# One pass over the second chunk, modulation from PSUM on ACT, and early products of a second FFN group

## The chip, the cores and the metric

The kernel runs on one core of a Trainium2 chip. The metric is the time of one execution on the device in microseconds (us), given as the median of several executions. The core has five engines that matter here: PE (TensorE, matrix products), DVE (VectorE), ACT (ScalarE), POOL (GpSimd) and SP (SyncE, which issues the loads). Each engine runs its own queue in order; semaphores between the engines make an instruction wait for its inputs and for a free buffer.

## The reference, cut to what matters

Two layers work on 1024 rows of 1024 values. Layer 0 mixes the rows by differential attention, layer 1 by centred averages over 2, 4, 8 and 16 neighbours. After each mixer comes a SwiGLU feed-forward network (FFN) with 2816 hidden values. Each of the four sub-layers modulates its input by a scale and a shift, is gated, added to its input and normalised.

```python
def modulate(h, shift, scale):
    return h * (1 + scale) + shift

def swiglu(h, w_in, w_out):
    g, u = jnp.split(h @ w_in, 2, axis=-1)
    return (jax.nn.silu(g) * u) @ w_out

for i in range(DEPTH):
    sh1, sc1, g1, sh2, sc2, g2 = adaln_params(c[:, None, :], w_mod[i], b_mod[i])
    hx = modulate(x, sh1, sc1)
    # y_lat: attention with w_o (layer 0), multiscale_pool(hx, pool_w, pool_scale) (layer 1)
    x = layer_norm(ALPHA * x + g1 * y_lat, ln_g[i, 0], ln_b[i, 0])
    x = layer_norm(ALPHA * x + g2 * swiglu(modulate(x, sh2, sc2), w_in[i], w_out[i]),
                   ln_g[i, 1], ln_b[i, 1])
```

## The kernel before

The state x lies transposed in SBUF as `zT`: 8 tiles of 128 features by 1024 rows. The rows are handled in two chunks of 512. Every fp32 product is made of three fp32r matmuls (`mm3`): an operand is cut into a high part, a cast on ACT (L386), and a remainder, a subtraction on DVE or POOL (L387); `parts` does both. Weights come by DMA into a ring `raw` of RAW = 4 buffers and are cut into a ring `aop` of AOP = 3 by `form`. `ct` is a ring of CT = 5 buffers for partial results, `quad` one of QD = 4.

After attention the stages follow one another:

- w_o, the attention's output product (`w_o`, L677 to L707). The first chunk is one pass of 512 columns over 8 output tiles d; the second is two passes of 256, each with its own weight forms.
- FFN of layer 0 (`ffn`, L709 to L874), in 11 groups of 2 x 128 hidden values. Both chunks are multiplied together by a Strassen-like scheme with 7 products per half (p0 to p6, gate half s = 0 and linear half s = 1), each of 12 matmuls of 512 columns. Their inputs H[0] to H[6] are seven forms of the modulated x: H[0] and H[1] come from the first chunk alone, the others also from the second chunk. At the end of a group 16 output products of 6 matmuls each add its share to zT. In group 0 and in the last group the two halves go product by product (p0 of both, then p1 of both, ...); in the others half after half.
- pooling (`pool_group`), again one pass of 512 and two of 256, with 4 groups each; then the FFN of layer 1, and the last norm.

Between a mixer and its FFN the rows are normalised (`ln_rows`): PE transposes 128 rows (L558), DVE takes mean and variance, POOL the power (L564), ACT writes the normalised rows `xn` (L568). `features` transposes them back (L587), `to_x` writes x into zT on ACT (L591), `modulated` makes the modulated h from zT on DVE (L595), and `put` cuts a form into its parts. Of the second chunk, row tiles 4 and 5 are handled in the mixer's last pass (`second_x`, `forms_rest`), tiles 6 and 7 in group 0 between p0 and p1; `forms_4` and `forms_last` complete the forms in group 0. `beside(g)` puts a vector-matrix product for layer 1's modulation (`gemv`, 4 loads, 8 DVE operations and 4 matmuls) at the end of a group.

What stands first on an engine's queue is settled when the kernel is built, from the order of the code and the rings of buffers; nothing is reordered at run time.

Of the kernel before, what the change touches and what calls it, by code (L numbers as in the profile page):

```python
# [19 lines left out]
P = 128  # L20
# [18 lines left out]
RAW, AOP, CT, QD = 4, 3, 5, 4  # L39
# [4 lines left out]
def backbone(ctx: ExitStack, tc: tile.TileContext, a: dict, out: bass.AP):  # L44
# [78 lines left out]
    with ExitStack() as actx:  # L123
# [420 lines left out]
    def quad(dt=F32R):  # L544
        return pf.tile([P, 2, 512], dt, name="quad", tag="quad", bufs=QD)
# [51 lines left out]
    def put(H, i, s, cs, t, eng=None):  # L597
        parts(H[s][:, i, cs], H[s][:, 4 + i, cs], t, eng)

    def forms_first(li, M, H, rows, ks):  # L600

        if not H:
            H += [h_form(0), h_form(1), phx.tile([P, KT, 512], F32, name="h", tag="x0"), None, None, None, None]
        for k in ks:
            to_x(k, chunk[0], li, features(rows, k))
            modulated(H[2][:, k, :], k, chunk[0], M)
            put(H, k % 4, k // 4, chunk[0], H[2][:, k, :], G)

    def second_x(li, rows, t0, ks=range(KT)):

        for k in ks:
            to_x(k, slice(512 + t0, 512 + t0 + 256), li, features(rows, k))

    def forms_rest(M, H, t0, idx):

        if H[5] is None:
            H[5:7] = [h_form(s) for s in range(5, 7)]
        cs, zs = slice(t0, t0 + 256), slice(512 + t0, 512 + t0 + 256)
        for i in idx:
            k = i + 4  # L620
            t2, h21 = H[2][:, i, cs], H[2][:, k, cs]
            t = quad(F32)
            h12, h22, t4 = t[:, 0, 0:256], t[:, 0, 256:512], t[:, 1, 0:256]
            modulated(h12, i, zs, M)
            modulated(h22, k, zs, M)
# [3 lines left out]
            G.tensor_tensor(t4, h21, t2, ALU.subtract)  # L629
            put(H, i, 5, cs, h12)  # L630
            put(H, i, 6, cs, t4, G)

    def forms_4(H):
        H[4] = h_form(4)
        for i in range(4):
            put(H, i, 4, chunk[0], H[2][:, i, :])

    def forms_last(M, H):

        H[3] = h_form(3)  # L640
        ts = [quad(F32) for _ in range(4)]
        for i, t in enumerate(ts):
            modulated(t[:, 0], i + 4, chunk[1], M)
            V.tensor_tensor(t[:, 1], t[:, 0], H[2][:, i, :], ALU.subtract)
            put(H, i, 3, chunk[0], t[:, 1])
        H[2] = h_form(2)
        for i, t in enumerate(ts):
            put(H, i, 2, chunk[0], t[:, 0], G)
# [6 lines left out]
    def ffn_mod(l):  # L655

        return one_plus(l, 4, f"m1_{l}"), modv[l][:, 24:32]
# [18 lines left out]
    M0 = ffn_mod(0)  # L676
# [21 lines left out]
    for d in range(KT):  # L698
        w_o(d, 512, 256)
        if d >= 2:  # L700
            forms_first(0, M0, H, rows, [range(0, 2), range(2, 4), [4], [5], [6], [7]][d - 2])
    rows = rows_of(4, 6)
    for d in range(KT):
        w_o(d, 768, 256)
        if 1 <= d < 5:
            second_x(0, rows, 0, (d - 1, d + 3))
            forms_rest(M0, H, 0, [d - 1])  # L707

    def ffn(l, gate, li, M, H, beside=None, after=None):  # L709
        class Half:  # L710


            def __init__(self, j0, s, sg):
                self.s, self.sg = s, sg
                self.r0, self.r1 = [raw([P, KT, P]) for _ in range(2)]
                for i, r in enumerate((self.r0, self.r1)):
                    SP.dma_start(r, a["w_in"][l, j0 + i, :, s])
# [94 lines left out]
        for g in range(G2):  # L812
            last = g == G2 - 1
            sg = []
            if g == 0 or last:
# [4 lines left out]
                if not last:  # L820
                    second_x(li, rows_of(6, 8), 256)
                sg0 = ct()
                o = [h.p1_(ct() if h.s else None, sg0) for h in both][1]
                if last:
                    keep = phh.tile([P, 2, 2, 512], F32R, name="keep", tag="H0")
                    for j in range(2):
                        S.copy(keep[:, j], at[1][j])
                else:
                    forms_rest(M, H, 256, range(4))
                    forms_4(H)  # L830
                for h in both:
                    h.sums(G if last else V)
                for h in both:
                    h.p4()
                for h in both:
                    h.p5()
                if not last:
                    forms_last(M, H)
                sg += [quad(F32), quad(F32)]
                at = [both[0].at(o)]  # L840
                for f in (Half.p6, Half.p3, Half.p2):
                    at.append([f(h) for h in both][1])
            else:
                sg += [quad(F32), quad(F32)]
                for s in range(2):
                    h = Half(2 * g, s, sg)
                    h.p0()
                    h.sums()
                    h.p4()
                    at = [h.p1_(h.p1)]  # L850
                    h.p5()
                    at += [h.p6(), h.p3(), h.p2()]
# [32 lines left out]

    ffn(0, g2, 0, M0, H, beside=lambda g: gemv(1, g + 2) if g < 10 else None, after=ln_to_pool)

# [4 lines left out]
    M2 = ffn_mod(1)  # L892
# [5 lines left out]
    def pool_group(t0, n, g):  # L898
        wr = raw([P, 2, 256])
        SP.dma_start(wr, a["pool_w"][g].rearrange("(i p) o -> p i o", p=P))  # L900
        if n == 512:
            pt = phx.tile([P, 6, 512], F32R, name="pt", tag=f"x{g % 3}")
        elif t0 == 512:
            pt = phx.tile([P, 6, 512], F32R, name="pt", tag=f"x{1 + g % 2}")
        else:
            pt = [pwt.tile([P, 2, 512], F32R, name="pt", tag="aop", bufs=AOP) for _ in range(2)]
        if t0 == 768:
            w2, hl = pt[0], pt[1].rearrange("p s (i t) -> p (s i) t", i=2)
        else:
            w2, hl = pt[:, 0:2], pt[:, 2:6]  # L910
# [36 lines left out]
    rows = []  # L947
# [12 lines left out]

# [94 lines left out]
```

## Time and profile before

| | us |
|---|---|
| median of 3 runs (2364.8 to 2369.83) | 2365.12 |
| the profiled execution | 2363.8 |
| its span, first to last instruction | 2362.0 |
| PE busy in it | 2258.1 (96%) |
| DVE busy | 1691.5 (72%) |
| ACT busy | 933.0 (40%) |
| POOL busy | 615.5 (26%) |

The mean granted clock of TensorE is 0.984 of full speed. Of the chain that ended last, PE has 84%, DVE 10%, ACT, DMA, POOL and issue 1% each. Matmuls are pipelined, so a matmul's own duration is longer than the distance from its start to the next one's start; the distance is what counts. A busy share is a mean over stages with different limits, so the stages are to be read one by one.

### The profile page before, as it was taken

The page shows a single profiled execution, that of the slowest core. Times are in us where ns is not written, and L with a number is a line of the kernel's source. Part 1 is how long each engine was busy: PE and PEld are TensorE (multiplying, and loading weights), DVE is VectorE, ACT ScalarE, POOL GpSimd, SP SyncE. Part 2 cuts the span into 40 slices and gives each one's busy share as a digit, 9 for nine tenths or more (in the row PEclk, how much of TensorE's full clock was granted, in tenths as well). Part 3 has the DMA queues.
Part 4 walks back from the last instruction along what each step waited for, and adds up shares of the span by engine and source line. Part 5 has one row for each costly group of instructions (what it writes and reads, how often), then busy time and mean ns, then how long its engine had stood idle before and what let it go on. Part 6 is the DMA issues. An engine that isn't in the chain of part 4 may idle for free.

```text
span 2362.0 us, 31120 instructions
## 1 busy us (share of the span) xinstructions
PE 2258.1 (96%) x11832; PEld 1922.8 (81%) x11832; DVE 1691.5 (72%) x2572; ACT 933.0 (40%) x1635; POOL 615.5 (26%) x618
## 2 busy tenths in 40 slices
PE   5989999999999987999999999998799999999997
PEld 4868887999998876888888888897588888888886
DVE  6663626998996689777777777757966666666678
ACT  3213115788885453222222222447522222222242
POOL 3531312444443143111111111103421111111122
PEclk9999999999999998999999999999899999999999
DMA  7866745323222532222222222212111111111121
GB/s 285 270 206 216 232 134 161 110 82 87 84 57 78 172 99 90 88 82 89 90 89 89 89 81 90 79 34 77 36 54 55 54 49 51 54 54 53 48 88 72
DMA packets 101350, 236.64 MB, mean 100 GB/s; under 512 B 9424, under 2 KB 27472, under 8 KB 100176
## 3 DMA queue, kind: packets, MB, share of 16 engines
q1 hardware_dynamic: 79120, 210.53, 27.6%
q10 hardware_dynamic: 22080, 24.12, 3.6%
q8 instruction: 93, 1.52, 0.2%
q14 instruction: 57, 0.47, 0.1%
HBM read 206.30 MB, written 28.31 MB: 99 GB/s over the span
## 4 chain that ended last, share of the span: by engine, by line
PE 84%; DVE 10%; ACT 1%; DMA 1%; issue 1%; POOL 1%; SPq 0%; DVEq 0%; ACTq 0%; POOLq 0%
PE mm L667 18%; PE mm L666 18%; PE mm L665 18%; PE s L424 6%; PE misc L455 6%; PE misc L448 3%; PE mm L171 3%; PE mm L170 3%; PE mm L169 3%; PE mm L160 1%; PE mm L161 1%; PE mm L159 1%; DVE aop L387 1%; DVE zT L670 1%; PE mm L928 1%
## 5 line engine op out<-in xcount | busy, mean ns | idle before, releaser
L665 PE MATMUL mm<-H,aop 128*128 128x512 f32 x1232 | 484.0, 393 | 18.0 <-ACT aop L386 10.5
L667 PE MATMUL mm<-H,aop 128*128 128x512 f32 x1232 | 482.2, 392 | 7.3 <-DVE aop L387 7.3
L386 ACT CAST aop<-raw 128x512 fp32r<-128x512 f32 x392 | 241.8, 621 | 620.9 <-PE mm L667 568.5
L666 PE MATMUL mm<-H,aop 128*128 128x512 f32 x1232 | 483.3, 392 | 3.3 <-DVE H L387 3.3
L670 DVE SCALAR_TENSOR_TENSOR zT<-mm,g,zT 128x512 f32<-128x512 f32 (+1 forms) x400 | 276.7, 703 | 122.7 <-PE mm L667 120.6
L387 DVE TENSOR_TENSOR aop<-raw,aop 128x512 fp32r<-128x512 f32 x392 | 279.3, 715 | 102.0 <-ACT aop L386 100.9
L665 PEld LDWEIGHTS mm<-H,aop 128*128 128x128 f32 x1232 | 233.1, 189 | 68.7 <-ACT aop L386 13.2
L667 PEld LDWEIGHTS mm<-H,aop 128*128 128x128 f32 x1232 | 233.1, 189 | 58.1 <-DVE aop L387 10.2
L666 PEld LDWEIGHTS mm<-H,aop 128*128 128x128 f32 x1232 | 233.1, 189 | 52.4 <-DVE H L387 4.5
L666 PE MATMUL mm<-quad,aop 128*128 128x512 f32 x608 | 237.7, 391 | 2.0 <-DVE quad L387 1.9
L665 PE MATMUL mm<-quad,aop 128*128 128x512 f32 x608 | 237.6, 391 | 0.1
L667 PE MATMUL mm<-quad,aop 128*128 128x512 f32 x608 | 236.2, 389 | 0.0
L427 DVE TENSOR_REDUCE mx<-s 128x1 f32<-128x1280 f32 x128 | 190.7, 1490 | 40.1 <-PE s L424 35.2
L424 PE MATMUL s<-kk,qd 128*128 128x512 f32 (+1 forms) x768 | 184.2, 376 | 4.9 <-DMA qd<-q_d 2.8
L430 ACT ACTIVATE e<-s,mx 128x1280 f32<-128x1280 f32 x128 | 170.0, 1328 | 26.0 <-DVE mx L427 26.0
L742 POOL TENSOR_TENSOR raw<-s,raw 128x512 f32<-128x512 f32 x40 | 52.0, 1299 | 452.0 <-DVE aop L387 322.4
L424 PEld LDWEIGHTS s<-kk,qd 128*128 128x128 f32 x768 | 137.6, 193 | 30.0 <-issue 3.5
L455 PE MATMUL misc<-vv,at 128*128 128x128 f32 x1280 | 153.5, 275 | 0.6 <-ACT at L449 0.6
L433 POOL TENSOR_SCALAR e<-e,sm 128x1280 f32<-128x1280 f32 x64 | 88.1, 1376 | 248.0 <-DVE sm L431 248.0
L455 PEld LDWEIGHTS misc<-vv,at 128*128 128x128 f32 x1280 | 148.0, 192 | 0.8 <-ACT at L449 0.8
L666 PEld LDWEIGHTS mm<-quad,aop 128*128 128x128 f32 x608 | 114.2, 188 | 28.7 <-DVE quad L387 5.7
L665 PEld LDWEIGHTS mm<-quad,aop 128*128 128x128 f32 x608 | 114.2, 188 | 24.3 <-ACT aop L386 0.8
(175 smaller groups left out, 4086.8 us busy)
## 6 DMA issues: line engine op xcount, KB each, us to landing
gw<-in_w_mod SPq DMA_DIRECT2D x96, 512.0 KB, 4.5
raw<-in_w_in SPq DMA_DIRECT2D x88, 512.0 KB, 3.6
raw<-in_w_out SPq DMA_DIRECT2D x48, 512.0 KB, 3.4
qd<-q_d SPq DMA_DIRECT2D x64, 256.0 KB, 5.7
raw<-in_w_o SPq DMA_DIRECT2D x24, 512.0 KB, 4.1
kk<-k_d SPq DMA_DIRECT2D x8, 1280.0 KB, 6.9
wr<-in_w_qk SPq DMA_DIRECT2D x18, 512.0 KB, 5.8
k_d<-ot ACTq DMA_DIRECT2D x32, 256.0 KB, 4.2
```

The costliest lines, as they stand in the source:

```text
L169: PE.matmul(ps[:, 0:n], lhsT=wh[:, k, :], rhs=hi, start=(k == 0), stop=False)
L386: S.copy(hi, src)
L387: (eng or V).tensor_tensor(lo, src, hi.bitcast(F32), ALU.subtract)
L424: PE.matmul(ps[:, lo_:hi_], lhsT=self.qd[:, m, s, q0:q0 + P], rhs=self.kk[:, m, lo_:hi_], start=(s == 0), stop=(s == 1))
L427: V.tensor_reduce(mx, ps[:, 0:TA], axis=AX.X, op=ALU.max, negate=True)
L430: S.activation(e, ps[:, 0:TA], AF.Exp, bias=mx, accum_out=sm)
L433: G.tensor_scalar(e, e, sm, 1.0, ALU.mult, ALU.mult)
L455: PE.matmul(av, lhsT=self.at[:, kb, :], rhs=self.vv[:, kb, :], start=(kb == 0), stop=(kb == NTT - 1))
L665: PE.matmul(p_, lhsT=wh, rhs=xh, start=first, stop=False)
L666: PE.matmul(p_, lhsT=wh, rhs=xl, start=False, stop=False)
L667: PE.matmul(p_, lhsT=wl, rhs=xh, start=False, stop=last)
L670: V.scalar_tensor_tensor(zT[:, d, cs], p_, gate[:, d:d + 1], zT[:, d, cs], ALU.mult, ALU.add)
```

## The change

- w_o's second chunk and pooling's second chunk are each one pass of 512 columns.
- The modulation moves from DVE (from zT) to ACT (from PSUM, beside `to_x`); layer norm's gain and bias are folded into its scale and bias (`ffn_mod`).
- All four row tiles of the second chunk are handled in group 0, behind p0 (`forms_second`).
- The products p0 and p1 of group 1 ("early") run in group 0, between p1 and p4; group 1 begins with p4.
- p2 runs ahead of p3, and p3 gives the last two results.
- The gemv of `beside` at g now makes part g + 1 (before: g + 2); none at g = 0, two (6 and 11) at g = 5. RAW is 6, CT is 8.

```diff
-RAW, AOP, CT, QD = 4, 3, 5, 4
+RAW, AOP, CT, QD = 6, 3, 8, 4
...
-    def modulated(dst, k, cs, M):
-        m1, sh = M
-        V.tensor_scalar(dst, zT[:, k, cs], m1[:, k:k + 1], sh[:, k:k + 1], ALU.mult, ALU.add)
+    def modulated(dst, k, p_, M):
+        gm, bm = M
+        S.activation(dst, p_, AF.Identity, bias=bm[:, k:k + 1], scale=gm[:, k:k + 1])
...
+    def forms_second(li, M, H):
+        rows = rows_of(4, 8)
+        H[3] = phh.tile([P, KT, 512], F32, name="hB", tag="H3")
+        H[5:7] = [h_form(s) for s in range(5, 7)]
+        for i in range(4):
+            for k in (i, i + 4):
+                p_ = features(rows, k)
+                modulated(H[3][:, k, :], k, p_, M)
+                to_x(k, chunk[1], li, p_)
+            t2, h21, h12, h22 = H[2][:, i, :], H[2][:, i + 4, :], H[3][:, i, :], H[3][:, i + 4, :]
             V.tensor_tensor(t2, h12, t2, ALU.subtract)
             V.tensor_tensor(t2, h22, t2, ALU.subtract)
             G.tensor_tensor(h12, h22, h12, ALU.subtract)
...
+            G.tensor_tensor(h21, h21, t2, ALU.subtract)
         H[4] = h_form(4)
         for i in range(4):
...
+            put(H, i, 4, H[2][:, i, :])
+        for i in range(4):
+            put(H, i, 5, H[3][:, i, :])
+        for i in range(4):
+            put(H, i, 6, H[2][:, i + 4, :], G)
...
     for d in range(KT):
-        w_o(d, 512, 256)
-        if d >= 2:
-            forms_first(0, M0, H, rows, [range(0, 2), range(2, 4), [4], [5], [6], [7]][d - 2])
-    rows = rows_of(4, 6)
-    for d in range(KT):
-        w_o(d, 768, 256)
-        if 1 <= d < 5:
-            second_x(0, rows, 0, (d - 1, d + 3))
-            forms_rest(M0, H, 0, [d - 1])
+        w_o(d, 512, 512)
+        forms_first(0, M0, H, rows, [d])
...
+            def p2(self):
+                p_ = self.product(2, self.r0[:, 4:8])
+                V.tensor_tensor(self.u2, p_, self.u2, ALU.add)
+
             def p3(self):
                 p_ = self.product(3, self.s1.rearrange("p (i e) -> p i e", i=4))
-                V.tensor_tensor(self.u2, p_, self.u2, ALU.add)
-                return self.result(2, p_, self.u3, self.u3)
-
-            def p2(self):
-                p_ = self.product(2, self.r0[:, 4:8])
-                return self.result(3, p_, self.u2, self.u2)
+                return [self.result(2, p_, self.u3, self.u3), self.result(3, p_, self.u2, self.u2)]
...
                 if not last:
-                    second_x(li, rows_of(6, 8), 256)
+                    forms_second(li, M, H)
...
-                    forms_rest(M, H, 256, range(4))
-                    forms_4(H)
+                    early = [Half(2, s, None, False) for s in range(2)]
+                    for h in early:
+                        h.p0()
+                    early_sg = ct()
+                    early_o = [h.p1_(ct() if h.s else None, early_sg) for h in early][1]
...
+                    if g == 1:
+                        h = early[s]
+                        h.sg, h.r1 = sg, h.load(1)
+                        h.sums()
+                        h.p4()
+                        at = [h.at(early_o)] if s else [None]
...
     for g in range(4):
-        rows += rows_of(g, g + 1)
-        pool_group(512, 256, g)
-    for g in range(2):
-        pool_group(768, 256, g)
-        forms_first(2, M2, H, rows, range(4 * g, 4 * g + 4))
-    rows = rows_of(4, 6)
-    for g in range(2, 4):
-        pool_group(768, 256, g)
-        second_x(2, rows, 0, range(4 * g - 8, 4 * g - 4))
-    forms_rest(M2, H, 0, range(4))
+        pool_group(512, 512, g)
+        forms_first(2, M2, H, rows, range(2 * g, 2 * g + 2))
```

Lines of the kernel after stand some rows lower: the high and low part stay at L386 and L387, `modulated` is L596, the result's copy L731, its sum and product L777 and L778, zT's update L673.

The first place is ACT's queue in group 0 of layer 0, from the normalised rows on. In the kernel before (H_7996, H_7997 and H_8472 are forms 5, 6 and 4, `ct<-ct` is silu of the first gate result):

```order
L568 ACTIVATE xn<-ln,nb,mv 128x512 x4
L591 ACTIVATE zT<-ln,lnb,lng 128x256 x8
L774 ACT_TABLE_LOAD
L774 ACTIVATE ct<-ct 128x512
L386 CAST H_7996<-quad 128x256
L386 CAST H_7997<-quad 128x256
```

In the kernel after (H_8087, H_8013 and H_8014 are forms 4, 5 and 6; the rows begin behind seven pairs like the first two, and the copies in the row before the last are those of early p0):

```order
L596 ACTIVATE hB<-ln,bm_7139,gm_7137 128x512
L591 ACTIVATE zT<-ln,lnb,lng 128x512
L386 CAST H_8087<-h 128x512 x4
L386 CAST H_8013<-hB 128x512 x4
L386 CAST H_8014<-h 128x512 x4
L731 COPY ct<-mm 128x512 x2
L386 CAST aop<-raw 128x512 x3
```

Eight activations of 256 have become sixteen of 512, in eight pairs, and the first weight form of early p1, which leads the last row, stands behind the casts of twelve tiles of forms 4 to 6. Silu and its table load stand ahead of all pairs.

The second place is DVE's queue at the end of a regular group of layer 0. In the kernel before (`quad<-ct` is the remainder of a result, `modv` the gemv's result):

```order
L776 TENSOR_TENSOR ct<-mm,ct 128x512
L387 TENSOR_TENSOR aop<-raw,aop 128x512
L777 TENSOR_TENSOR ct<-ct,quad 128x512
L776 TENSOR_TENSOR ct<-mm,ct 128x512
L118 TENSOR_TENSOR modv_79<-pg,bmod 128x4
L777 TENSOR_TENSOR ct<-ct,quad 128x512
L387 TENSOR_TENSOR quad<-ct,quad 128x512
L387 TENSOR_TENSOR aop<-raw,aop 128x512
L387 TENSOR_TENSOR quad<-ct,quad 128x512
L670 SCALAR_TENSOR_TENSOR zT<-mm,g_0_7439,zT 128x512 x2
```

In the kernel after:

```order
L763 TENSOR_TENSOR ct<-mm,ct 128x512
L387 TENSOR_TENSOR aop<-raw,aop 128x512
L777 TENSOR_TENSOR ct<-mm,ct 128x512 x2
L778 TENSOR_TENSOR ct<-ct,quad 128x512 x2
L118 TENSOR_TENSOR modv_79<-pg,bmod 128x4
L387 TENSOR_TENSOR quad<-ct,quad 128x512 x2
L673 SCALAR_TENSOR_TENSOR zT<-mm,g_0_7443,zT 128x512 x3
```

The sums, products and remainders of the last two results, which were apart, stand in pairs, and the weight remainder stands ahead of them.

## Rows read from the trace of the kernel before

**Rows 1.** Busy time by stage. Columns: window, its length, each engine's busy time, clock, DMA.

```profile
802.60:869.00 66.40, 60.95 (x482) 57.17 (x481) 56.14 (x107) 42.73 (x76) 27.77 (x26) 1.00 0.39 122
869.00:928.10 59.10, 46.62 (x203) 36.04 (x201) 55.07 (x88) 29.57 (x55) 21.20 (x20) 0.88 0.17 55
952.30:1012.60 60.30, 60.30 (x272) 50.08 (x270) 44.48 (x67) 16.97 (x28) 10.98 (x8) 1.00 0.27 88
1593.50:1646.20 52.70, 46.69 (x369) 44.17 (x367) 40.76 (x90) 41.17 (x77) 16.71 (x17) 0.94 0.29 87
1646.20:1710.90 64.70, 47.54 (x184) 35.23 (x185) 61.13 (x95) 30.95 (x62) 30.27 (x30) 0.82 0.10 33
```

**Rows 2.** The same view, the slow stretch of each group 0.

```profile
888.00:901.60 13.60, 6.26 (x13) 4.23 (x14) 13.27 (x20) 5.72 (x14) 8.10 (x9) 0.51 0.00 1
...
1669.00:1686.50 17.50, 7.45 (x15) 4.69 (x16) 16.27 (x23) 6.78 (x15) 10.44 (x12) 0.52 0.01 1
```

**Rows 3.** PE's waits, w_o's second chunk and group 0 of layer 0: total, times, longest.

```profile
PE mm L665 <- ACT H L386: 7.6, 1, 7.6
...
PE mm L666 <- DVE H L387: 3.3, 1, 3.3
```

**Rows 4.** PE's waits, second pooling chunk and group 0 of layer 1.

```profile
PE mm L665 <- ACT aop L386: 10.5, 5, 6.4
PE mm L667 <- DVE aop L387: 5.9, 2, 3.5
```

**Rows 5.** PE's waits, regular groups of layer 1.

```profile
PE mm L666 <- DVE quad L387: 1.9, 8, 0.7
```

**Rows 6.** PE's timeline: start, duration, instruction, count; end of w_o to layer norm.

```profile
869.11 0.28 PE L667 MATMUL mm<-onH,aop 128*128 128x256 f32 x1
869.23 0.40 PE L665 MATMUL mm<-H,aop 128*128 128x512 f32 x1
...
874.70 1.80 PE L558 MATMUL ln<-ident,zT 128*128 128x128 f32 x15
876.26 0.48 PE L665 MATMUL mm<-H,aop 128*128 128x512 f32 x1
```

**Rows 7.** ACT's timeline, group 0 of layer 0.

```profile
879.17 2.79 ACT L568 ACTIVATE xn<-ln,nb,mv 128x512 f32<-128x512 f32 x4 [3.16 <-DVE nb L566]
...
885.62 1.28 ACT L774 ACT_TABLE_LOAD   x1
...
909.26 2.71 ACT L386 CAST H<-quad 128x512 fp32r<-128x512 f32 x5 [1.39 <-DVE quad L644]
```

**Rows 8.** ACT's groups by form, 754 to 1000: busy us, mean ns, idle before.

```profile
L591 ACT ACTIVATE zT<-ln,lnb,lng 128x512 f32<-128x512 f32 x8 | 6.0, 778 | 0.0
```

**Rows 9.** POOL's groups by form, the same stretch.

```profile
L387 POOL TENSOR_TENSOR H<-h,H 128x512 fp32r<-128x512 f32 x8 | 11.1, 1401 | 16.4 <-ACT H L386 16.4
```

**Rows 10.** DVE's groups by form, the same stretch.

```profile
L595 DVE TENSOR_SCALAR h<-zT,m,modv 128x512 f32<-128x512 f32 x8 | 4.2, 535 | 0.1
L387 DVE TENSOR_TENSOR H<-quad,H 128x512 fp32r<-128x512 f32 x4 | 3.8, 962 | 0.0
...
L644 DVE TENSOR_TENSOR quad<-quad,h 128x512 f32<-128x512 f32 x4 | 2.6, 682 | 0.0
```

**Rows 11.** PE's timeline, zero and bands of one pooling group.

```profile
1589.46 0.47 PE L922 MATMUL mm<-zero_r 128*128 128x512 f32 x1
...
1590.87 0.71 PE L665 MATMUL mm<-pt 128*128 128x512 f32 x2
```

**Rows 12.** DVE's timeline, end of a group in layer 1.

```profile
1831.55 1.78 DVE L777 TENSOR_TENSOR ct<-ct,quad 128x512 f32<-128x512 f32 x1
...
1836.98 0.67 DVE L387 TENSOR_TENSOR quad<-ct,quad 128x512 fp32r<-128x512 f32 x1
```

**Rows 13.** PE's timeline, the same place.

```profile
1831.48 0.39 PE L667 MATMUL mm<-H,aop 128*128 128x512 f32 x1
...
1837.71 0.50 PE L666 MATMUL mm<-quad,aop 128*128 128x512 f32 x1 [0.18 <-DVE quad L387]
```

More of the change, by code (lines that the diff above doesn't have):

```diff
@@ L604, in forms_first @@
         for k in ks:
[L605 to L625, printed above, removed]
+            p_ = features(rows, k)
+            modulated(H[2][:, k, :], k, p_, M)
+            to_x(k, chunk[0], li, p_)
+            put(H, k % 4, k // 4, H[2][:, k, :], G)
+    def forms_second(li, M, H):
[4 more added lines that the diff above has]
+            for k in (i, i + 4):
+                p_ = features(rows, k)
+                modulated(H[3][:, k, :], k, p_, M)
+                to_x(k, chunk[1], li, p_)
+            t2, h21, h12, h22 = H[2][:, i, :], H[2][:, i + 4, :], H[3][:, i, :], H[3][:, i + 4, :]
             V.tensor_tensor(t2, h12, t2, ALU.subtract)
@@ L628, in forms_rest, with forms_last @@
             G.tensor_tensor(h12, h22, h12, ALU.subtract)
[L629 to L633, printed above, removed]
+            G.tensor_tensor(h21, h21, t2, ALU.subtract)
         H[4] = h_form(4)
         for i in range(4):
-            put(H, i, 4, chunk[0], H[2][:, i, :])
-    def forms_last(M, H):
-        H[3] = h_form(3)
[L641 to L648, printed above, removed]
+            put(H, i, 4, H[2][:, i, :])
[3 more added lines that the diff above has]
+            put(H, i, 6, H[2][:, i + 4, :], G)
+    def forms_last(H):
+        t1 = [quad(F32) for _ in range(2)]
+        t1 = [t[:, j] for t in t1 for j in range(2)]
+        for i in range(4):
+            V.tensor_tensor(t1[i], H[3][:, i + 4, :], H[2][:, i, :], ALU.subtract)
+        hB = H[3]
+        H[2] = h_form(2)
+        for i in range(4):
+            put(H, i, 2, hB[:, i + 4, :], G if i % 2 else V)
+        H[3] = h_form(3)
+        for i in range(4):
+            put(H, i, 3, t1[i])
     def one_plus(l, ci, name):
@@ L698, in backbone, with __init__, load @@
     for d in range(KT):
-        w_o(d, 512, 256)
-        if d >= 2:
-            forms_first(0, M0, H, rows, [range(0, 2), range(2, 4), [4], [5], [6], [7]][d - 2])
-    rows = rows_of(4, 6)
-    for d in range(KT):
-        w_o(d, 768, 256)
-        if 1 <= d < 5:
-            second_x(0, rows, 0, (d - 1, d + 3))
-            forms_rest(M0, H, 0, [d - 1])
+        w_o(d, 512, 512)
+        forms_first(0, M0, H, rows, [d])
     def ffn(l, gate, li, M, H, beside=None, after=None):
         class Half:
[L713 to L717, printed above, removed]
+            def __init__(self, j0, s, sg, both=True):
+                self.j0, self.s, self.sg = j0, s, sg
+                self.r0 = self.load(0)
+                if both:
+                    self.r1 = self.load(1)
+            def load(self, i):
+                r = raw([P, KT, P])
+                SP.dma_start(r, a["w_in"][l, self.j0 + i, :, self.s])
+                return r
             def product(self, s, src):
@@ L834, in ffn @@
                     h.p4()
+                at = [both[0].at(o)]
                 for h in both:
@@ L837, in ffn @@
                 if not last:
-                    forms_last(M, H)
+                    forms_last(H)
                 sg += [quad(F32), quad(F32)]
-                at = [both[0].at(o)]
-                for f in (Half.p6, Half.p3, Half.p2):
-                    at.append([f(h) for h in both][1])
+                at.append([h.p6() for h in both][1])
+                for h in both:
+                    h.p2()
+                at += [h.p3() for h in both][1]
             else:
@@ L884, in ln_to_pool, with beside @@
                 ln_rows(t, xr[t // 4][:, t % 4, :])
-    ffn(0, g2, 0, M0, H, beside=lambda g: gemv(1, g + 2) if g < 10 else None, after=ln_to_pool)
+    def beside(g):
+        for b in {0: (), 5: (6, 11), 10: ()}.get(g, (g + 1,)):
+            gemv(1, b)
+    ffn(0, g2, 0, M0, H, beside=beside, after=ln_to_pool)
     A1 = one_plus(1, 1, "A1")
@@ L900, in pool_group @@
         SP.dma_start(wr, a["pool_w"][g].rearrange("(i p) o -> p i o", p=P))
[L901 to L910, printed above, removed]
+        pt = phx.tile([P, 6, 512], F32R, name="pt", tag=f"x{g % 3 if t0 == 0 else 1 + g % 2}")
+        w2, hl = pt[:, 0:2], pt[:, 2:6]
         wh, wl = [w2[:, i, :].rearrange("p (i o) -> p i o", i=2) for i in range(2)]
@@ L946, in backbone @@
             ln_rows(6 + g, xr[1][:, 2 + g, :])
[L947 removed]
+    rows = rows_of(0, 4)
     for g in range(4):
[L949 to L958 removed]
+        pool_group(512, 512, g)
+        forms_first(2, M2, H, rows, range(2 * g, 2 * g + 2))
     gb, xo = [], []
```

33 lines of the change are left out of this document (20 added, 13 removed).

## The prediction

> **What bounds the kernel now.** I first read busy time by stage, cutting the span where PE changes its work [rows 1]. The rows are, in order: the second half of w_o, group 0 of the first FFN, a regular FFN group, the second chunk of pooling, and group 0 of the second FFN. In a regular group PE is busy for all 60.30 us; nothing can be gained there unless PE gets less work. The other four stages, 242.9 us together, are where PE stands still or runs slowly: group 0 has PE busy for 46.62 of 59.10 us in layer 0 and 47.54 of 64.70 in layer 1, and the granted clock is 0.88 and 0.82. Next I cut both group 0s finer [rows 2]: the low mean comes from one stretch each, at 0.51 and 0.52, the lower of the clock's two levels (1.2 of 2.4 GHz), where PE is busy less than half of the time. Then the waits of PE. In w_o and group 0 of layer 0, two waits, for the ACT cast and the DVE remainder of forms of h, hold it for 7.6 and 3.3 us [rows 3]; in layer 1 the waits stand at weight forms queued behind forms of h (10.5 and 5.9 us, [rows 4]). In the groups of layer 1 a small wait returns: 1.9 us in 8 for the last activation piece [rows 5].
>
> **Unit prices.** A 512-column matmul follows the one before by 5.47/24 = 0.228 us, a 256-column one by 0.12, and 16 transposes take 1.56 us, 0.10 each (869.23 to 874.70 to 876.26, [rows 6]). ACT activations of 512 from PSUM follow each other by (2.79 − 0.78)/3 = 0.67, casts by (2.71 − 0.62)/4 = 0.52, and the table load takes 1.28 [rows 7, 8].
>
> **The change part by part.**
>
> *A, w_o, second chunk.* Before: 384 matmuls of 256, 46.1 us, and 97 transposes, 10.1: 56.2 of 66.40 us, so 10.2 were lost. After: 192 matmuls of 512, 43.8, and 64 transposes (the second chunk's go to group 0), 6.7: 50.5. ACT and DVE make half as many weight forms, so both have room. I add 1.5 for the first layer norm, whose rows are needed early: 52.0, −14.4. Bounds: nothing lost, −15.9; the old 10.2 lost again, −5.7.
>
> *B, group 0 of layer 0.* All four second-chunk row tiles are now handled here, and every result goes through ACT's queue, in order. From the stage's start: p0 takes 24 × 0.228 = 5.5; normalised rows follow the first transpose by 4.5 (874.70 to 879.17, [rows 6, 7]): 10.0. Four activations 2.7, table load 1.3, silu and one weight cast 1.1: 15.1. The other two row tiles, 2.7: 17.8, and I take 18.3 since POOL's power step stands between. Then 16 activations from PSUM (modulated and plain x), 16 × 0.67 = 10.7: 29.0. Twelve casts of forms of h at 0.52 = 6.3: 35.3. Two result copies and the cast of early p1's weights, 1.6: 36.9. DVE's remainder 0.7: 37.6. Early p0 needs nothing from the chain's end, so PE covers until about 26, but early p1 has to wait although its data (form 1 of h) was there from the start: its weight cast is queued behind all of that. So PE idles about 11 us, and I take it that the clock falls as it does before: there PE worked 6.26 us at half speed [rows 2], so 3.1 were lost. Then 144 matmuls, 32.8: 37.6 + 3.1 + 32.8 = 73.5. Two early products leave group 1, 48 × 0.228 = 10.9: net 62.6 against 59.10: **+3.5**. Bounds: no idle time, PE work 216 × 0.228 + 64 × 0.10 = 55.6 − 10.9 = 44.7, −14.4; POOL holding the casts, +9 (its eight subtractions, at 1.4 each as for its remainders [rows 9], would end at 40 if they began at 29.0, and the first of its four remainders stand behind them).
>
> One thing speaks against putting the modulation here. An activation of 512 from PSUM takes ACT 778 ns [rows 8]; the modulation took DVE 535 ns from SBUF [rows 10]. The Trainium skill, "ScalarE: Activation LUTs", section "Rules for kernel authors", sends additions and multiplications to VectorE, not ScalarE, and the rows agree. By that rule, with the eight modulations left on DVE, ACT's chain would be 8 × 0.67 = 5.4 us shorter in each group 0, and the whole sum 10.8 lower; the change doesn't follow it, and the sum above has ACT's price.
>
> *C, second chunk of pooling.* Four passes of 512 for eight of 256. PE's work: 48 matmuls 10.9; 64 feature transposes and 32 of layer norm 10.0; eight times zero and bands at 1.41 (1589.46 to 1590.87, [rows 11]) 11.3: 32.2. ACT decides: its normalised rows end at about 14.5 (4.5 behind, four pairs, two weight casts between), then its queue holds 26 activations and 7 casts up to p0's first weight form: 17.4 + 3.6 = 21.0, 35.5; DVE 0.7, the last ten matmuls 2.3, 0.6 to the first product: 39.1 against 52.70: **−13.6**. Bounds: PE's work alone, −20.5; as much lost as before (52.7 less some 40.6 of work, 12.1), 44.3, −8.4.
>
> *D, group 0 of layer 1.* The chain of B without the table load: 73.5 − 1.3 = 72.2, less 10.9: 61.3 against 64.70: **−3.4**. Bounds −20.0 (44.7) and +5.
>
> *E, ends of groups.* p2 moves ahead of p3, and p3 gives the last two results together. Before, the last remainder ends at 1836.98 + 0.67, 6.0 after the last product's end (1831.48 + 0.23), while 24 output matmuls cover 5.5 [rows 12, 13]; the next one starts at 1837.71. After, DVE does two additions, two products, two remainders: 6 × 0.6, with 0.4 to start and about 0.5 for ACT's cast: 4.5. Covered: the 1.9 us of [rows 5] go. Bounds −3.6 (with the start delays behind these waits) and the two rivals below.
>
> *F, the rest at nothing.* The gate vectors' loads move by a group, group 5 does two; DVE is idle 15.8 of 60.30 in a regular group [rows 1], and eight multiply-adds below 1 us each fit. If not, up to 3 us. More raw and ct buffers only let loads and results go earlier. The folded constants are 128x8 operations, done once.
>
> Sum: −14.4 + 3.5 − 13.6 − 3.4 − 1.9 = −29.8. The profiled execution took 2363.8 (span 2362.0), so 2334.0; the median of runs is 1.3 higher: **2335**.
>
> **The rivals.**
>
> *R1, the early products do cover the forms.* For: forms, activations and early weights are independent work, and 48 more matmuls stand there. Against: ACT's queue order, in which early p1's casts stand behind the twelve. Both group 0s would come to 44.7: −14.4 − 14.4 − 13.6 − 20.0 − 1.9 = −64.3, 2301 with the 1.3 for the median, as in all of these.
>
> *R2, the pair of results stretched by POOL.* Remainders on DVE took 962 ns beside POOL's work, plain subtractions 682 [rows 10]. If the six DVE operations at the end and the weight remainder ahead of them all run so, 7 × 0.28 = 2.0: 4.5 + 2.0 against a cover of 5.5, 1.0 in each of 20 groups: 2355. Against: at the group end shown one multiplication of the seven took 1.78 us [rows 12], 1.1 too long, and the last remainder 0.67, undisturbed; a stretch of all seven is not seen. The Trainium skill, "GPSIMD Engine Reference", section "Key points", says that POOL shares its SBUF interfaces with VectorE and contends with DVE instructions that have two SBUF inputs; these are five of the seven, so by that the stretch would be 1.4 at most, 0.4 a group, and the time 2343.
>
> *R3, slower than before.* The place is the same; the price is that the doubled result comes on top of the 6.0 observed rather than replacing it: four more operations at 0.68 = 2.7, 8.7 − 5.5 = 3.2 in each of 20 groups, 64, and E's 1.9 is not gained: 2401. It decides from 30/20 = 1.5 us per group on. For: before, one late result already overran the cover. Against: before, a weight remainder stood between the two late results, and an accumulation between product and remainder; these move behind.
>
> *R4, the waits stay in w_o and pooling.* One pass of 512 halves the number of forms but the same layer norm stands ahead, and its rows come through the same two engines; against it, ACT is busy for 42.73 of 66.40 us in w_o [rows 1], and the forms that go free eight casts and more: A −5.7, C −8.4, 13.9 more than the forecast: 2349.
>
> **How the numbers follow.** Forecast 0.60: 2335; R1 0.10, R2 0.12, R3 0.05, R4 0.13. The range takes 18 on either side of the forecast, about half of the way to the bounds of B and D together (−17.9 and −16.6 from their values below, +5.5 and +8.4 above) and what A and C can lose, and reaches into R4: 2317 to 2352. R1, R3 and some of R2 are left out. A measurement of this kernel can tell 0.2%, 4.7 us; only R3 is slower than that, and a bad R2 (with both group 0s at +5 to +9) falls within it: faster 0.90, same 0.05, slower 0.05.
>
> **What would show it.** In the second chunk of w_o PE runs through, in 52 us. In group 0 PE waits about 11 us for early p1's weight form, with ACT busy all the time, and the clock at half behind it. Group 1 is 11 us shorter. Pooling's second chunk takes 39 us, with waits on ACT. No wait on the last pieces at the ends of groups. I am wrong if group 0 shows no long wait (R1), or if the regular groups get longer (R2, R3).

## The result, and the profile after

The changed kernel takes 2378.0 us (median of 4 runs, 2376.7 to 2378.6) where the kernel before takes 2365.0 on the same chip: 1.0051 times as long, 95% interval 1.0034 to 1.0068. It is slower by half a percent; 2335 was forecast. The profiled execution has a span of 2376.8 us, 14.8 more than before.

Where the 14.8 us are, by the places at which PE changes its work in both traces (the products of H and the output products can be told apart by their operands):

| stretch | before | after | difference | forecast |
|---|---|---|---|---|
| start to the first w_o product | 754.09 | 764.45 | +10.4 | 0 |
| w_o, both chunks | 114.90 | 99.67 | −15.2 | −14.4 |
| H products of groups 0 and 1, layer 0 | 98.01 | 107.75 | +9.7 | +3.5 |
| their output products | 46.04 | 44.12 | −1.9 | 0 |
| groups 2 to 10, layer 0 | 513.17 | 526.13 | +13.0 | 0 |
| pooling, with the last outputs of layer 0 | 120.05 | 106.55 | −13.5 | −13.6 |
| groups 0 and 1 of layer 1 | 147.12 | 151.37 | +4.3 | −3.4 |
| groups 2 to 10, layer 1, up to the last outputs | 509.78 | 516.19 | +6.4 | −1.9 |
| the end | 58.8 | 60.6 | +1.7 | 0 |

The two passes of 512 came out as forecast. Nearly all the rest is worse, and the largest part lies in the regular groups of both layers, where the change leaves the number of products as it was: 19 us.

There the products themselves are slower. The busy time by stage (columns as in [rows 1]) for the H products of one regular group of layer 1, of the kernel before:

```profile
1853.70:1891.80 38.10, 38.10 (x169) 31.53 (x168) 21.01 (x32) 13.46 (x22) 4.36 (x4) 1.00 0.19 56
```

And of the kernel after:

```profile
1861.00:1900.20 39.20, 39.20 (x169) 31.42 (x168) 21.41 (x31) 13.31 (x22) 9.64 (x7) 1.00 0.18 55
```

PE is busy without a gap in both, at full clock, with the same 169 matmuls: 38.10/168 = 0.2267 us from one to the next before, 39.20/168 = 0.2333 after. Only matmuls that read H (or the attention's output onH) are slower; those that read `quad` are not, as the costliest groups show (busy us, mean ns of one). In the kernel before:

```profile
L665 PE MATMUL mm<-H,aop 128*128 128x512 f32 x1232 | 484.0, 393 | 18.0 <-ACT aop L386 10.5 <-ACT H L386 7.6
L666 PE MATMUL mm<-quad,aop 128*128 128x512 f32 x608 | 237.7, 391 | 2.0 <-DVE quad L387 1.9
```

In the kernel after:

```profile
L668 PE MATMUL mm<-H,aop 128*128 128x512 f32 x1232 | 489.5, 397 | 24.8 <-ACT aop L386 24.8
L670 PE MATMUL mm<-H,aop 128*128 128x512 f32 x1232 | 488.7, 397 | 8.7 <-DVE aop L387 8.7
L669 PE MATMUL mm<-H,aop 128*128 128x512 f32 x1232 | 488.5, 397 | 0.0
L668 PE MATMUL mm<-quad,aop 128*128 128x512 f32 x608 | 237.7, 391 | 1.1 <-DVE zT L673 1.1
```

In the group 0 of layer 0 the waits of PE in the kernel after answer to [rows 3]:

```profile
PE mm L668 <- ACT aop L386: 12.4, 1, 12.4
PE mm L670 <- DVE aop L387: 4.3, 1, 4.3
```

The first is the wait that was forecast (about 11 us for early p1's weight form). The second was not. ACT's timeline of that stretch (start, duration, instruction, count), with early p1's cast as the first of the last row:

```profile
893.13 1.77 ACT L386 CAST H<-h 128x512 fp32r<-128x512 f32 x3
...
898.13 2.17 ACT L386 CAST H<-h 128x512 fp32r<-128x512 f32 x4
900.21 1.06 ACT L731 COPY ct<-mm 128x512 f32<-128x512 f32 x2
901.16 1.66 ACT L386 CAST aop<-raw 128x512 fp32r<-128x512 f32 x3
```

DVE's timeline, with early p1's remainder as the first of the last row:

```profile
895.41 5.71 DVE L387 TENSOR_TENSOR H<-h,H 128x512 fp32r<-128x512 f32 x4
901.04 5.69 DVE L387 TENSOR_TENSOR H<-hB,H 128x512 fp32r<-128x512 f32 x4
906.66 1.88 DVE L387 TENSOR_TENSOR aop<-raw,aop 128x512 fp32r<-128x512 f32 x3
```

POOL's timeline beside it:

```profile
896.59 1.71 POOL L626 TENSOR_TENSOR h<-h 128x512 f32<-128x512 f32 x1
898.88 6.70 POOL L387 TENSOR_TENSOR H<-h,H 128x512 fp32r<-128x512 f32 x4 [0.59 <-ACT H L386]
```

And the busy time of the slow stretch, as in [rows 2]:

```profile
888.20:901.00 12.80, 1.22 (x7) 0.73 (x6) 12.59 (x9) 12.18 (x22) 12.21 (x9) 0.68 0.00 1
901.00:910.00 9.00, 3.83 (x8) 2.62 (x9) 9.00 (x11) 2.34 (x5) 4.59 (x3) 0.50 0.00 0
```

The stage begins at 864.12, so ACT begins early p1's cast at 901.16 − 864.12 = 37.0; the forecast had it done at 36.9. But the matching remainder on DVE comes only at 906.66, behind eight remainders of forms 4 and 5 that take 1.42 us each (5.71/4) beside POOL, not 0.6 to 0.7. And when PE resumes, after a wait of 12.4 us, the granted clock is 0.50 from 901 to 910, the lower level.

At the ends of groups the wait of [rows 5] is gone: the trace after has no wait of PE in the regular groups of layer 1, and their output products take 21.78 us instead of 22.25.

### The profile page after: what moved, and what is told of

Same layout as the page of the kernel before. It is cut to its first block, busy times and chain, and to the rows that moved or that the text cites. A ratio compares the mean times of both kernels' runs of the same rounds, so it can differ in the third digit from the quotient of the medians.

```text
span 2376.8 us, 30334 instructions
## 1 busy us (share of the span) xinstructions
PE 2273.1 (96%) x11552; PEld 1904.2 (80%) x11552; DVE 1642.8 (69%) x2458; ACT 928.9 (39%) x1599; POOL 603.3 (25%) x590
## 4 chain that ended last, share of the span: by engine, by line
PE 89%; DVE 6%; ACT 2%; DMA 1%; issue 1%; POOL 1%; SPq 0%; DVEq 0%; POOLq 0%; ACTq 0%
PE mm L670 20%; PE mm L668 20%; PE mm L669 20%; PE s L424 6%; PE misc L455 6%; PE misc L448 3%; PE mm L171 3%; PE mm L170 3%; PE mm L169 3%; PE mm L160 1%; PE mm L161 1%; PE mm L159 1%; DVE H L387 1%; DVE st L559 1%; PE mm L940 1%
## 5 line engine op out<-in xcount | busy, mean ns | idle before, releaser
L386 ACT CAST aop<-raw 128x512 fp32r<-128x512 f32 x376 | 232.6, 621 | 732.2 <-PE mm L670 662.6
L668 PE MATMUL mm<-H,aop 128*128 128x512 f32 x1232 | 489.5, 397 | 24.8 <-ACT aop L386 24.8
L670 PE MATMUL mm<-H,aop 128*128 128x512 f32 x1232 | 488.7, 397 | 8.7 <-DVE aop L387 8.7
L669 PE MATMUL mm<-H,aop 128*128 128x512 f32 x1232 | 488.5, 397 | 0.0
L387 DVE TENSOR_TENSOR aop<-raw,aop 128x512 fp32r<-128x512 f32 x376 | 268.1, 716 | 130.8 <-ACT aop L386 129.6
L673 DVE SCALAR_TENSOR_TENSOR zT<-mm,g,zT 128x512 f32<-128x512 f32 (+1 forms) x384 | 271.9, 722 | 83.2 <-PE mm L670 80.4
L670 PEld LDWEIGHTS mm<-H,aop 128*128 128x128 f32 x1232 | 231.9, 188 | 66.8 <-DVE aop L387 10.1
L741 POOL TENSOR_TENSOR s<-raw 128x512 f32<-128x512 f32 x40 | 53.2, 1330 | 454.7 <-DMA raw<-in_w_in 420.6
```

The source lines that it names most:

```text
L386: S.copy(hi, src)
L387: (eng or V).tensor_tensor(lo, src, hi.bitcast(F32), ALU.subtract)
L668: PE.matmul(p_, lhsT=wh, rhs=xh, start=first, stop=False)
L669: PE.matmul(p_, lhsT=wh, rhs=xl, start=False, stop=False)
L670: PE.matmul(p_, lhsT=wl, rhs=xh, start=False, stop=last)
L673: V.scalar_tensor_tensor(zT[:, d, cs], p_, gate[:, d:d + 1], zT[:, d, cs], ALU.mult, ALU.add)
```

## Experiments

Two theories came from this comparison. **Address**: buffers are laid out in SBUF from two sides, constants, rings, weight forms and `quad` from the left, H, x and zT from the right. The two folded constants (`bm_0` and `bm_1`, 32 B per partition each) move everything behind them on the left by 64 B, and a matmul whose moving operand (H) and weights (`aop`) no longer lie alike is slower. In the built program `aop` begins at byte 35584 = 139 × 256 of each partition before, and at 28480 = 111 × 256 + 64 after, while H stays at 163584 = 639 × 256. The change also cuts the scratch for dynamic DMA from 16384 to 1024 B per partition, which the list of the change above leaves out: `aop` lies 15360 lower by it, 8192 higher by two more buffers of raw and 64 higher by the constants. The first two are multiples of 256, so within 256 B only the constants move it. **Contention**: POOL's subtractions stretch DVE's chain in group 0. The rival to the first is the new order or the larger rings, the rival to the second a mere lack of time on DVE. All times are medians of 4 runs; the kernel before stayed between 2364.8 and 2365.9 beside them. a_pad, with which the later ones are compared, was run on another chip than those from c_under on, so a difference of about 1 us says nothing.

**a_pad**, the address alone.

```diff
     ident = ctile([P, P], "ident")
+    ctile([P, 48], "pad")
```

> The changed kernel with an unused tile of 192 B per partition among the constants, so that weight forms, quads and all buffers on the left side of SBUF begin at a multiple of 256 B again, as before the change (two new constants of 32 B had moved them by 64 B past one); H keeps its place. Theory address: each of the 3696 matmuls of H by aop and 384 of onH by aop goes from 0.2333 back to 0.2267 us, 27 us in all: 2378 - 27 = 2351, and 168 products of a regular group take 38.1 us, not 39.2. Rival order: the matmuls are slower because of the new order or the larger rings; then 39.2 stays, 2378.

Measured 2348.6, 0.9934 (0.9919 to 0.9949) of the kernel before, 29.4 us below the changed kernel. With 192 unused bytes the change is faster than the kernel before. The H products are back at the old rate (group of matmuls as above):

```profile
L669 PE MATMUL mm<-H,aop 128*128 128x512 f32 x1232 | 483.2, 392 | 24.8 <-ACT aop L387 24.8
```

The waits stayed, the mean fell from 397 to 392 ns, and the H products of a regular group of layer 1 take 38.08 again. Of the 30.7 us between the two profiled executions 24.2 lie in the stretches of w_o and of the groups; 4.7 lie before the first w_o product and are another loss (see Open).

**b_shift**, the same the other way, on the kernel before.

```diff
     ident = ctile([P, P], "ident")
+    ctile([P, 16], "pad")
```

> The kernel before with an unused tile of 64 B among the constants, nothing else. Theory address: 168 products of a regular group go from 38.1 to 39.2 us, 25 us over 22 groups, 1 to 3 more in w_o: about 2391. If the 64 B also cost the start of the kernel its 4.6 us, 2395. Rival order: 2365, nothing changes.

Measured 2388.1, 1.0102 (1.0087 to 1.0117). 64 unused bytes cost the old kernel 23 us, with 39.20 us for the H products of a regular group of layer 1; order and rings have no part in it. Its group of matmuls:

```profile
L666 PE MATMUL mm<-H,aop 128*128 128x512 f32 x1232 | 489.9, 398 | 18.1 <-ACT aop L387 10.5 <-ACT H L387 7.6
```

**a_edge**, H moved to the weights' place instead.

```diff
-EDGE = 224
+EDGE = 416
```

> The changed kernel with the pad on the right side of SBUF at 416 B instead of 224, so that H and x tiles lie at 64 B past a multiple of 256 B, as the weight forms do. Theory relative address (the moving operand and the weights must have the same place within 256 B): 2351, 38.1 us a group. Rival absolute address (each has to begin at a multiple of 128 or 256 B): 39.2 us a group or more, 2378 or above.

Measured 2350.6, 0.9939 (0.9922 to 0.9955), mean 392 ns. Both operands lie at 64 B past a multiple of 256 here, and the rate is the fast one: what counts is how they lie to each other, not each by itself. The left side was moved as a whole against the right; that the matmul's own two operands matter follows from the matmuls of `quad` by `aop`, which lie on the same side and kept 391 ns in all these runs. Only differences of a multiple of 256 B and of 64 B more were tried, so 256 as the period is not shown.

**a_pad_wo4**, fewer early loads (on a_pad, as all that follow).

```diff
-        wo_raw = [raw_o(d) for d in range(RAW)]
+        wo_raw = [raw_o(d) for d in range(4)]
```

> The changed kernel with the 192 B pad and 4 loads of w_o ahead of attention instead of 6 (the ring raw has 6 buffers in both). Theory queue: the two loads more stand ahead of attention's k and q loads in SP's queue and make its first matmul late by 5.5 us: 5 us less than the kernel with the pad alone. Rival: the first loads of attention are late for another reason (DMA traffic, v written back); no difference from the pad alone.

Measured 2348.3: no difference. The theory falls; the first load of k went out at 365.94, no earlier than with six loads. SP's queue in the changed kernel gives another reason, the last matmul of qkv (waits: total, times, longest):

```profile
SPq L107 <- DVE aop L387: 13.3, 1, 13.3
SPq L498 <- PE mm L161: 6.6, 1, 6.6
```

L498 loads attention's k. Raw has grown by 2 × 4 KB, and so `kk` lies on bytes that qkv's weight tiles still hold: in the built program its first buffer is at bytes 40768 to 51008 and the first weight tile (`wh`) begins at 44864; before, they were at 47872 to 58112 and at 60160.

**c_under**, which puts qkv's buffers back where they were.

```diff
+        under = actx.enter_context(tc.tile_pool(name="under", bufs=1))
+        under.tile([P, 15104 // 4], F32, name="under", tag="under")
```

> As the changed kernel with the 192 B pad (2348.6), with an unused tile of 15104 B below the buffers of the qkv stage alone, which puts these where they lay before the change, while attention's k and q buffers stay where they are. Theory overlap: the larger ring raw (8 KB more) had pushed attention's k buffer onto weight tiles that the last qkv matmuls still read, so its first load waits for them; with the tile the load goes out some 5 us earlier and attention starts 5 us earlier: 2343. Rival queue: the load waits behind loads into the ring raw; nothing changes, 2348.6.

Measured 2344.2, 4.4 below a_pad. The load of k no longer waits for that matmul; the first load of q behind it still does, for 6.1 us, so part of the delay is left: PE's wait ahead of the first product of attention is 3.7 us, 7.8 in a_pad and 2.2 in the kernel before. Issue of the load of k in the changed kernel (SP's timeline):

```profile
362.25 0.38 SPq L107 DMA_DIRECT2D gw<-in_w_mod  x1
369.29 0.38 SPq L498 DMA_DIRECT2D kk<-k_d  x1
```

The same in c_under, right behind the load ahead of it:

```profile
358.26 0.38 SPq L108 DMA_DIRECT2D gw<-in_w_mod  x1
358.68 0.47 SPq L501 DMA_DIRECT2D kk<-k_d  x1
```

**c_late**, forms 4 to 6 issued behind the early products.

```diff
+    def forms_put(H):
         H[4] = h_form(4)
...
                     early_o = [h.p1_(ct() if h.s else None, early_sg) for h in early][1]
+                    forms_put(H)
...
```

> As the changed kernel with the 192 B pad, with the casts and remainders of forms 4, 5 and 6 issued behind the early products' weight forms. Theory: in each group 0 the early p1 was late by ACT's twelve casts (12.4 us of wait) and then by DVE's eight remainders of 1.42 us (4.3 more); with its weight form first, PE resumes some 6 to 11 us earlier and the remainders lie beside the 5.5 us of early p1: 16 to 22 us less over two layers, 2327 to 2333. Rival: the forms themselves are what ends last (DVE's chain), so PE only waits at p4 instead of early p1: 2348.

Measured 2341.4, 7.2 below a_pad, less than half of what was expected. In group 0 of layer 0 PE now waits 5.5 us for early p1, then 3.0 more for p4's weight form, which stands behind the twelve casts.

**c_noearly**, without the early products.

```diff
-                    early = [Half(2, s, None, False) for s in range(2)]
-                    for h in early:
-                        h.p0()
...
-                    if g == 1:
+                    if g == -1:
...
```

> As the changed kernel with the 192 B pad, without the early products: group 1 does all its products itself. Theory: standing behind the forms' casts, the early products cover only the 5.5 us of early p0, and PE then waits for early p1 longer than it would for form 4: without them the kernel loses nothing, 2343 to 2349. Rival: they do cover the forms; then leaving them out costs up to 10.9 us in each layer, 2360 to 2370.

Measured 2352.3, 3.7 above a_pad, above the first range and far below the rival's. Of 2 × 10.9 us of products that moved into group 0, the change gains 3.7: its early products cover a sixth. Both expected ranges were missed.

**c_p3p2**, p3 ahead of p2 with one result each, as before the change.

> As the changed kernel with the 192 B pad, with p3 ahead of p2 and one result from each, as before the change. Theory: the wait of 0.47 us at the end of each group of layer 1 comes back, eight groups and group 0, 4 us: 2352.5. Rival (the reorder does nothing, the wait went with the buffers): 2348.6.

Measured 2355.4, 6.8 above a_pad. The regular groups of layer 1 go back to 22.24 us for their outputs (0.47 us in each of groups 2 to 8, 3.3 in all); the output products of group 0 of layer 0 take 3.7 more, where the theory had one wait of 0.47.

**d_mod**, the modulation on DVE, from PSUM.

```diff
-        S.activation(dst, p_, AF.Identity, bias=bm[:, k:k + 1], scale=gm[:, k:k + 1])
+        V.tensor_scalar(dst, p_, gm[:, k:k + 1], bm[:, k:k + 1], ALU.mult, ALU.add)
```

> As the changed kernel with the 192 B pad (2348.6), with the modulation on DVE, from PSUM, where the change has ACT do it. Theory: in group 0 ACT's queue is what early p1 waits for, so eight activations less on it (5.4 us) bring its weight form forward by 3 to 5 us in each layer, and DVE's eight more operations cost back at most as much: 2340 to 2349. Rival: DVE's remainders end last, and eight more operations on DVE beside POOL make it later: 2350 to 2360.

Measured 2345.3, in the theory's range but not for its reason: the H products of group 0 take 77.14 us in layer 0 (76.97 in a_pad), since PE now waits 13.9 us for early p1's weight form, not 12.4. Pooling is 2.2 shorter. Group 0 gains nothing from ACT's eight activations less: its casts now wait for POOL's subtractions, 6.4 us in four waits, of which the longest two are (ACT's timeline):

```profile
885.97 0.62 ACT L387 CAST H<-hB 128x512 fp32r<-128x512 f32 x1 [2.31 <-POOL hB L626]
894.34 0.62 ACT L387 CAST H<-hB 128x512 fp32r<-128x512 f32 x1 [2.03 <-POOL hB L626]
```

**d_split**, each of forms 4 to 6 right ahead of its own product.

```diff
...
+                if not last:
+                    form_put(H, 4)
                 for h in both:
                     h.p4()
...
```

> As the kernel with the casts of forms 4 to 6 behind the early products' weight forms (2341.4), with each of these forms now issued right ahead of its own product. Theory: there, p4's weight form stood behind all twelve casts and a silu, a wait of 3.0 us in each group 0; it goes: 2334 to 2338. Rival: the remainders on DVE set p4 and p5 anyway: 2341.

Measured 2336.6, 4.8 below c_late. The wait of 3.0 us at p4 is gone in each layer, but the waits for weight remainders on DVE grow from 1.1 to 3.8 us in layer 0, so the H products of group 0 are 1.6 and 1.4 us shorter. 1.5 of the 4.8 lie before the first w_o product, which this edit doesn't touch.

**e_mid**, early p1 issued between the halves of the feature work.

```diff
...
+            if i == 1:
+                mid()
...
```

> As the kernel before in this list, with the early products' weight forms issued between the four normalised row tiles and the rest of the feature work (after two of four steps). Theory: PE has p0, p1, early p0 and early p1 (21.8 us) and the transposes to do while ACT makes its 16 activations, and then waits some 6 us for form 4 instead of 17 for early p1: 10 to 13 us less a layer than the kernel with the pad alone, 2323 to 2329. Rival: ACT's 16 activations begin that much later behind the early products, and the wait only moves from early p1 to p4: 2334 to 2341.

Measured 2339.1: the wait moved, as the rival said. In group 0 of layer 0 PE waits 5.7 us for weight remainders (the longest 2.6) and 2.5 for form 4's remainder, all on DVE.

**e_best**, the same with c_under's tile.

> The kernel with the early forms in the middle and, besides, the unused 15104 B below the qkv stage's buffers (4.4 us earlier start of attention when done alone). Theory: the two add up, 4 us below the kernel with the early forms in the middle, 2319 to 2325. Rival: the gain at attention is taken back by a later load in w_o; no difference.

Measured 2335.0, 4.2 below e_mid: c_under's gain adds up, but both stand 10 us above the expected ranges.

**f_dve**, POOL's part of the forms in group 0 on DVE, and nothing else changed against a_pad.

```diff
-            G.tensor_tensor(h12, h22, h12, ALU.subtract)
-            G.tensor_tensor(h21, h21, t2, ALU.subtract)
+            V.tensor_tensor(h12, h22, h12, ALU.subtract)
+            V.tensor_tensor(h21, h21, t2, ALU.subtract)
...
-            put(H, i, 6, H[2][:, i + 4, :], G)
+            put(H, i, 6, H[2][:, i + 4, :])
```

> As the changed kernel with the 192 B pad (2348.6), with all of POOL's subtractions and remainders of forms 5 and 6 in group 0 on DVE. Theory contention: DVE's operations there fall from 1.4 to 1.75 us to 0.7, so DVE ends no later although it does twelve more; the 4.3 us wait for early p1's remainder goes and part of the half-speed time with it: 2336 to 2344. Rival: DVE lacks the time; eight more subtractions of 0.7 push the forms and early p1 back by 5 us in each layer: 2354 to 2360.

Measured 2338.0, 0.9883 (0.9869 to 0.9898) of before, 10.6 below a_pad. Form 5's remainders were on DVE already; with eight subtractions and form 6's four remainders DVE has twelve operations of 128x512 more in each group 0 and is done earlier, by its timeline:

```profile
892.69 2.49 DVE L388 TENSOR_TENSOR H<-h,H 128x512 fp32r<-128x512 f32 x4
895.10 2.49 DVE L388 TENSOR_TENSOR H<-hB,H 128x512 fp32r<-128x512 f32 x4
897.51 2.49 DVE L388 TENSOR_TENSOR H<-h,H 128x512 fp32r<-128x512 f32 x4
899.91 1.89 DVE L388 TENSOR_TENSOR aop<-raw,aop 128x512 fp32r<-128x512 f32 x3
```

PE's waits in its group 0:

```profile
PE mm L669 <- ACT aop L387: 11.7, 1, 11.7
...
PE mm L671 <- DVE aop L388: 0.2, 1, 0.2
```

Four remainders take 2.49 us instead of 5.71, and the 4.3 us wait is gone. That is contention, not lack of time. The H products of group 0 are 4.2 us shorter than a_pad's in layer 0 and 6.3 in layer 1, about the whole gain.

**f_split** and **f_mid**: the two orders with POOL's part on DVE and c_under's tile.

> The kernel with each of forms 4 to 6 issued right ahead of its own product, behind the early weight forms (2336.6), with POOL's work in group 0 on DVE and the unused 15104 B below the qkv stage's buffers (4.4 us alone). Theory contention: 5 us less a layer and 4.4 less at attention: 2319 to 2326. Rival (lack of time on DVE): 2332 to 2342.

> The kernel with the early weight forms in the middle and the unused 15104 B (2335.0), with POOL's work in group 0 on DVE. Theory contention: DVE's remainders of form 4 come 4 to 6 us earlier in each layer: 2322 to 2328. Rival (lack of time on DVE): 2335 or above.

Measured 2323.2, 0.9822 (0.9806 to 0.9838) of before, and 2328.5, 0.9842 (0.9827 to 0.9857), half a microsecond above its range. f_split is the fastest of all, 42 us below the kernel before and 55 below the changed one. Its H products in group 0 of layer 0 take 65.48 us (78.94 in the changed kernel), with one long wait left:

```profile
PE mm L670 <- ACT aop L389: 5.5, 1, 5.5
```

## Why the prediction was wrong

**The step that failed** is the unit price, "A 512-column matmul follows the one before by 5.47/24 = 0.228 us", carried over to all H products of the kernel after, and with it the sum's lack of any term for the regular groups. 3696 matmuls of H and 384 of onH went from 0.2267 to 0.2333 us: 4080 × 0.0067 = 27 us by count. a_pad takes 29.4 away, of which its trace has 24.2 in the stretches of these products; b_shift adds 23.4 to the kernel before, and a_edge shows that it is the operands' place to each other. "The folded constants are 128x8 operations, done once" priced them by their work; their 64 bytes of SBUF were the cost. The table of buffers in the program would have told that everything on the left had moved by other than a multiple of 256 B, not what that costs: no row of the trace before shows it. a_pad, at 2348.6, lies within the stated range but 13.6 above the forecast. Its trace has 5.7 us more than forecast before the first w_o product, 10.1 in groups 0 and 1 (3.5 and 6.6) and 3.3 in the other groups of layer 0, less 5.3 where stages came out better; these are the smaller misses below.

**A, w_o: right.** The second chunk runs from 811.22 to 864.12, 52.9 us for the 52.0 forecast, of which 192 × 0.0067 = 1.3 are the slower matmuls. R4 did not come.

**B and D, the group 0s: mechanism right, one term mis-sized.** ACT's queue was forecast to within 0.7 us of 37. The step "DVE's remainder 0.7" was wrong: the remainder stood in DVE's queue behind eight others of 1.42 us. Without the address effect (a_pad) groups 0 and 1 cost +7.0 in layer 0 (76.97 + 28.00 against 59.12 + 38.89) and +2.9 in layer 1; with POOL's work gone (f_dve) +2.7 and −3.4, where +3.5 and −3.4 were forecast. So the difference is POOL's contention. The prediction had DVE stretched by POOL as R2, at the ends of groups only; in B, POOL stood only in the upper bound of +9, as holding up ACT's casts, and in the kernel after ACT does not wait for POOL anywhere between its sixteen activations and early p1's cast. The Trainium skill, "GPSIMD Engine Reference", section "Key points", says that POOL shares SBUF interfaces with VectorE and contends with DVE instructions of two SBUF inputs; the trace agrees, with 1.42 us beside POOL and 0.62 without it. Here both engines together were slower than DVE alone.

With the modulations on DVE the whole sum was to be 10.8 lower. d_mod puts them there and is 3.3 below a_pad, with next to nothing gained in either group 0 (77.14 and 77.99 us, 76.97 and 78.46 in a_pad): ACT's casts then wait for POOL's subtractions, which follow each other by 1.67 us. The Trainium skill, "ScalarE: Activation LUTs", section "Rules for kernel authors", gives additions and multiplications to VectorE; in group 0 the measurement differs from what that rule would give. Whether the rule pays once POOL's work is gone was not tried.

**R1** (early products cover the forms) is out: c_noearly shows that they are worth 3.7 us as placed. Placed ahead of the forms' casts, with each form ahead of its product and POOL's work on DVE, the same products leave 5.5 us of wait in f_split.

**C, pooling: right in size**, −13.5 for −13.6; the second chunk takes 39.0 us (1609.65 to 1648.67) for 39.1, and d_mod's 2.2 us less there fits ACT as the bound. But PE's waits on ACT there are 2.4 us, and from 1636 on ACT waits for PE in turn, so that ACT sets the whole length, as the sum had it, is not shown; the close agreement is partly luck.

**E, ends of groups: right in kind, too small.** 0.47 us in each of eight groups of layer 1 went, 3.8, twice the row's 1.9 and 0.2 past the bound of 3.6; the start delay behind a wait counts. c_p3p2 brings the wait back. R3 did not come, nor did R2 at the ends of groups.

**F: not nothing.** Group 5 of layer 0, with two gemv, has output products of 24.65 us instead of 21.86: 2.8, close to the bound given. DVE's multiply-adds for the gemv stand between zT's updates there, and PE waits 1.1 us for one of these.

**Not in the sum: attention's start.** The larger ring raw was priced as "only lets loads and results go earlier". It moved attention's k buffer onto weights in use; c_under gives 4.4 us of it back.

**Open.** The first 60 us of the kernel after lost 4.6 us to a late DVE sum and a granted clock of 0.50 behind it (57 to 63.4 us). In a_pad the first product of attention comes at 373.8 rather than 378.05, with the wait for k unchanged (6.6 us). a_edge, whose matmuls run at the fast rate, has the loss in part (granted clock 0.92 from 48 to 70 us; 0.84 in the kernel after, 0.99 in a_pad), so it does not hang on that rate; what decides it was not tried. Whether the effect of the operands' place goes with other differences than 64 B, and what in the engine makes it, was not tried either.

## What to carry to other kernels

When a change adds or resizes a buffer, look at where all the other buffers come to lie, both to each other (here 64 bytes cost some 24 us in matmuls that the change did not touch) and over what earlier stages still use. Follow a late operand through every engine that makes it: the cast was on time, its remainder was not. Work given to POOL beside a DVE chain can cost DVE more than doing it there.

## What the runs showed of the hardware

- fp32r matmuls of 128x512 follow each other by 0.2267 us when the starts of moving operand and weights differ by a multiple of 256 B, and by 0.2333 when they differ by 64 B more, at full granted clock (no other differences were tried).
- A DVE subtraction of 128x512 with both inputs in SBUF takes 0.62 us back to back alone (f_dve) and 1.42 beside POOL's, which take 1.7 each (the kernel after). Twelve operations moved from POOL to DVE made DVE finish earlier.
